# Folding the two half-masked key blocks of a windowed attention into one square

## The chip, the cores and the metric

The kernel runs on one core of a Trainium2 chip. The time is device time in microseconds; the kernel before took 1605.19 us (median of three runs, 1604.76 to 1605.27). One more execution was profiled; its trace is what is read below. Of the engines, TensorE (PE; its weight loads are PEld) multiplies matrices, VectorE (DVE), ScalarE (ACT) and GpSimd (POOL) do the rest, and SyncE (SP) issues the transfers.

## The reference

Two transformer blocks in sequence, over 512 tokens of width 2048, in float32. The change touches the first block's attention alone: 32 query heads of width 64 in 4 key groups (8 heads each), a window of 128 tokens, query blocks of 128 tokens, a bias by distance and a sink in the softmax:

```
kj = jnp.arange(2 * L)[None, :]           # L = 128: the key block before, and the own one
dist = qi + L - kj
in_band = (dist >= 0) & (dist < SWA_WINDOW)
s = jnp.einsum('bqhgd,bkhd->bhgqk', qj, kb) * scale + bias
s = jnp.where(in_band & (start - L + kj >= 0), s, -jnp.inf)
m = jnp.maximum(jnp.max(s, axis=-1, keepdims=True), sink)
p = jnp.exp(s - m)
p = p / (jnp.sum(p, axis=-1, keepdims=True) + jnp.exp(sink - m))
o = jnp.einsum('bhgqk,bkhd->bqhgd', p, vb)
```

For query i the window takes keys j <= i of the own block and keys j > i of the block before. So at each place (i, j) of a 128x128 square exactly one of the two blocks counts, and the other is masked.

## The kernel before

Every product is made of float32 numbers split in a high and a low half (`split`, lines 266 to 274: ACT writes the high half, VectorE the rest a moment later, as a "post"). Three matmuls (high x high, high x low, low x high) make one product.

Block 1 runs as one stream of projections on TensorE. `proj_n` goes over the 16 slices of 128 rows of a weight matrix; each step of three matmuls into one of four PSUM banks (`pj`) is a unit. The weights come in by DMA as `raw`, ACT converts them to `wh`, VectorE to `wl`, up to four slices ahead. First the projection of k and v (banks `kv_ps`), then four of q (`swa_q(g)`, from line 595, one for each key group), then the gate (`gate1(c)`).

The attention of group g is fed into the stream as pieces (`swa_pieces`, from line 638), so many for each unit (`F.rate`), while q of the next group is projected. An item is a group g, a query block t (0 to 3) and half of the heads (i): 32 items of 4 heads. Its pieces are: `s1` (twice: scores of two heads against 256 keys in a PSUM tile `sc`; VectorE adds the bias, takes the minimum `nm` and writes `p`; ACT takes exp and the row sum), `norm` (VectorE scales p by 1/sum), `s2` for each of the two key blocks (TensorE transposes four heads of p into a PSUM tile `tp`; the split makes `pth` and `ptl`), and `s3` (the products with v, bank `pv`, two matmuls a key block, the halves of v side by side; then the output goes to memory by DMA). `s3` of an item comes two pieces after its `s2`. At t = 0 there is only the own block.

The q of a group is normed after its bank is done (`evac`): ACT copies it (`qn`) and squares it, VectorE sums, GpSimd makes 1/sqrt (`rsqrt_mean`: `st`, a tensor_scalar and a pow) and multiplies (line 612). These are four norms for each group, one for each t; much later, ACT and VectorE split the result, TensorE transposes it, and `qt` is ready for `s1`.

ACT runs in the order of the program. For the other engines a scheduler lays the instructions in an order when the program is built; on the chip each engine then runs its own list in order and waits at whatever is not ready.

When the first bank of the gate is done (`gate1`, c = 0), all pieces that are left are issued, the attention's memory is closed, and the outputs are read back (`oin`) to be multiplied by the gate.

Of the kernel before, what the change touches and what calls it, by code (L numbers as in the profile page):

```python
# [9 lines left out]
F32 = mybir.dt.float32  # L10
# [10 lines left out]
NTB = 4  # L21
# [14 lines left out]
def mixer_kernel(ctx, tc, x, rel_bias, w_in1, q_gain, k_gain, sinks, w_out1,  # L36
# [483 lines left out]
    ktl = p1.tile([128, 4, S], F32R, name="ktl")  # L520
    vt = [p1.tile([128, 4, 2, 64], F32R, name=f"v{t}") for t in range(NTB)]

    def hstat():
# [7 lines left out]

    kn_all = p1.tile([128, 4, 256], F32, tag="p", name="kn_all", bufs=2)
    for t in range(NTB):
        ps = kv_ps[t]
        nc.scalar.activation(out=kn_all[:, t, :], in_=ps[:, 0:256], func=ACTF.Copy, scale=rstd1[:, t:t + 1])
        split(vt[t][:, :, 0, :], vt[t][:, :, 1, :], ps[:, 256:512].rearrange("p (g d) -> p g d", g=4),
              rstd1[:, t:t + 1])

    def k_norm(t):
        kn = kn_all[:, t, :]  # L540
        kn3 = kn.rearrange("p (g d) -> p g d", g=4)
        sq = qn_t()
        nc.scalar.activation(out=sq[:, :256], in_=kn, func=ACTF.Square)
# [94 lines left out]
    def swa_pieces():  # L638
# [3 lines left out]
        def s1(n, j):  # L642
# [20 lines left out]
            for a in range(2):  # L663
                b = 2 * j + a
                nc.vector.tensor_tensor_reduce(  # L665
                    out=p[:, b, :w], in0=sc[:, a, :w], in1=back(bias, b, w), scale=1.0,
                    scalar=nsink[:, h0 + b:h0 + b + 1], op0=ALU.add, op1=ALU.min,
                    accum_out=nm[:, b:b + 1])
                nc.scalar.activation(out=p[:, b, :w], in_=p[:, b, :w], func=ACTF.Exp, scale=-1.0,  # L669
                                     bias=nm[:, b:b + 1], accum_out=sm[:, b:b + 1])  # L670
# [6 lines left out]
        def norm(n):  # L677
            g, t, i = items[n]
            w = 128 if t == 0 else 256
            p, es, sm = st[n]["p"], st[n]["es"], st[n]["sm"]  # L680
            nc.vector.tensor_tensor(out=es, in0=es, in1=sm, op=ALU.add)
            nc.vector.reciprocal(out=es, in_=es)
            for b in range(4):
                nc.vector.tensor_scalar(out=p[:, b, :w], in0=p[:, b, :w], scalar1=es[:, b:b + 1],
                                        scalar2=None, op0=ALU.mult)

        def s2(n, kb):
            g, t, i = items[n]
            if kb == 0:
                st[n]["pth"] = p1.tile([128, 2, 512], F32R, tag="pth", name="pth", bufs=1)  # L690
                st[n]["ptl"] = p1.tile([128, 2, 512], F32R, tag="ptl", name="ptl", bufs=1)
            tp = tpt()
            for b in range(4):
                nc.tensor.transpose(tp[:, b, :], st[n]["p"][:, b, kb * 128:(kb + 1) * 128], ident)  # L694
            split(st[n]["pth"][:, kb, :], st[n]["ptl"][:, kb, :], tp.rearrange("p a b -> p (a b)"))

        def s3(n):
            g, t, i = items[n]
            h0 = 8 * g + 4 * i
            nk = 1 if t == 0 else 2  # L700
            k0 = max(t - 1, 0)
            pth, ptl = st[n]["pth"], st[n]["ptl"]
            o = ps_tp.tile([128, 512], F32, tag="tp", name="pv")
            for kb in range(nk):
                v = vt[k0 + kb][:, g].rearrange("p a b -> p (a b)")
                mm(o, v, pth[:, kb, :], kb == 0, False)
# [19 lines left out]
        for n in range(N + 2):  # L726
# [14 lines left out]
            if prev:  # L741
                out_p.append((None, lambda n=n: s2(n - 1, 0)))
            if prev and items[n - 1][1] > 0:
                out_p.append((None, lambda n=n: s2(n - 1, 1)))
        return out_p

    swa_bias(0)
    F.feed(swa_pieces())
    F.rate = 0.6
    for g in range(4):  # L750
# [43 lines left out]
    for t in range(NTB):  # L794
        F.defer(12 + t, lambda t=t: row_bcast(rb2[:, t * 128:(t + 1) * 128], rstd1[:, t:t + 1]))
    F.rate = 1.1
    phase({ACT})
# [789 lines left out]
```

## Time and profile before

| what | value |
|---|---|
| median of three runs | 1605.19 us (1604.76 to 1605.27) |
| the profiled execution | 1604.56 us, its span 1602.8 us |
| PE busy in the span | 1585.7 us, 99% |
| DVE, ACT, POOL busy | 917.8, 727.9, 110.1 us |
| chain that ended last | PE 91%, DVE 4%, ACT 2%, DMA 1%, issue 1% |
| granted TensorE clock | 0.999 of full speed |

The profile's page gives busy times of one execution. A matmul's own duration overlaps that of the next one; what a matmul adds to a full TensorE is the step from its start to the next start, which the chain of waits shows. A group of instructions is named by its line, engine, output and inputs. An "idle before" with a name says what the engine waited for.

### The profile page before, as it was taken

Reading aid. Unit: us, or ns where it says so; the run is one execution under the profiler, and the core shown is the slowest. Engines: PE = TensorE matmul, PEld = TensorE weight load, DVE = VectorE, ACT = ScalarE, POOL = GpSimd, SP = SyncE. Lnnn points to the kernel's source line nnn. Section 1 sums busy time; section 2 is a strip of 40 time slices with the busy share of each in tenths; the row PEclk is TensorE's granted clock in tenths of the full one; section 3 lists DMA queues with packets and bytes.
Section 4 is the critical chain, followed back from the end, with each engine's and each line's share of the span. In section 5 each row is a group of like instructions: output and inputs, shape, how many; then the busy total and the mean of one; then the engine's idle time right before and its main releaser. Section 6 shows DMA issues by size and latency. Waiting matters only on the chain.

```text
span 1602.8 us, 23242 instructions
## 1 busy us (share of the span) xinstructions
PE 1585.7 (99%) x8615; PEld 1358.8 (85%) x8615; DVE 917.8 (57%) x2218; ACT 727.9 (45%) x1608; POOL 110.1 (7%) x165
## 2 busy tenths in 40 slices
PE   9999999999999999999999999999999999999998
PEld 7788888887888788888899999999999888888887
DVE  6658888887454333333666766656657455455332
ACT  5556766775333323333455454545545333334322
POOL 3330320300000000000100000000000000000001
PEclk9999999999999999999999999999999999999999
DMA  6422323325333534342332322232232364365312
GB/s 231 146 79 83 104 81 96 84 69 171 120 104 104 161 123 142 110 134 67 80 96 67 92 71 79 74 86 76 57 106 66 109 203 127 95 221 173 105 40 106
DMA packets 144674, 173.78 MB, mean 108 GB/s; under 512 B 13088, under 2 KB 82080, under 8 KB 144032
## 3 DMA queue, kind: packets, MB, share of 16 engines
q1 hardware_dynamic: 144560, 172.29, 35.1%
q8 instruction: 68, 1.11, 0.3%
q14 instruction: 46, 0.38, 0.1%
HBM read 155.41 MB, written 16.84 MB: 107 GB/s over the span
## 4 chain that ended last, share of the span: by engine, by line
PE 91%; DVE 4%; ACT 2%; DMA 1%; issue 1%; POOL 0%; SPq 0%; ACTq 0%; POOLq 0%; DVEq 0%
PE pj L111 78%; PE sc L111 4%; PE pv L111 4%; PE tp L694 1%; PE tp L1290 1%; DMA xt<-in_x_t_dram 1%; DVE wl L168 1%; PE tp L622 1%; PE tp L425 0%; DVE xl L274 0%; PE sqs L1344 0%; PE ck_m L111 0%; ACT p L669 0%; DVE dql L272 0%; ACT wh L158 0%
## 5 line engine op out<-in xcount | busy, mean ns | idle before, releaser
L168 DVE TENSOR_TENSOR wl<-raw,wh 128x512 fp32r<-128x512 f32 (+1 forms) x488 | 336.0, 695 | 404.9 <-ACT wh L158 403.0
L158 ACT ACTIVATE wh<-raw 128x512 fp32r<-128x512 f32 (+1 forms) x488 | 298.6, 619 | 401.4 <-PE pj L111 351.4
L111 PE MATMUL pj<-xh,wh 128*128 128x512 f32 (+1 forms) x1152 | 363.6, 352 | 0.0
L111 PE MATMUL pj<-xh,wl 128*128 128x512 f32 (+1 forms) x1152 | 356.5, 345 | 0.6 <-DVE wl L168 0.6
L111 PE MATMUL pj<-xl,wh 128*128 128x512 f32 (+1 forms) x1152 | 356.3, 345 | 0.0
L111 PEld LDWEIGHTS pj<-xh,wh 128*128 128x128 f32 x1152 | 205.5, 188 | 27.8 <-ACT wh L158 0.4
L111 PEld LDWEIGHTS pj<-xh,wl 128*128 128x128 f32 x1152 | 199.7, 188 | 27.6 <-DVE wl L168 1.0
L111 PEld LDWEIGHTS pj<-xl,wh 128*128 128x128 f32 x1152 | 199.9, 188 | 19.5
L111 PE MATMUL pj<-wh,ogh 128*128 128x512 f32 (+1 forms) x528 | 204.6, 388 | 0.0
L111 PE MATMUL pj<-wl,ogh 128*128 128x512 f32 (+1 forms) x528 | 203.7, 386 | 0.0
L111 PE MATMUL pj<-wh,ogl 128*128 128x512 f32 (+1 forms) x528 | 203.6, 386 | 0.0
L111 PE MATMUL pj<-wh,xh 128*128 128x512 f32 (+1 forms) x448 | 175.3, 391 | 0.9 <-DVE v L274 0.7
L111 PE MATMUL pj<-wh,xl 128*128 128x512 f32 (+1 forms) x448 | 171.1, 382 | 1.2 <-DVE xl L274 1.1
L111 PE MATMUL pj<-wl,xh 128*128 128x512 f32 (+1 forms) x448 | 170.5, 380 | 0.1
L1253 ACT ACTIVATE p2t<-p2t,nm 128x144 f32<-128x144 f32 (+3 forms) x96 | 55.2, 575 | 140.0 <-DVE nm L1249 139.9
L111 PEld LDWEIGHTS pj<-wh,ogl 128*128 128x128 f32 x528 | 99.2, 188 | 21.3
L111 PEld LDWEIGHTS pj<-wh,ogh 128*128 128x128 f32 x528 | 99.2, 188 | 20.8
L111 PEld LDWEIGHTS pj<-wl,ogh 128*128 128x128 f32 x528 | 99.2, 188 | 20.7
L111 PEld LDWEIGHTS pj<-wh,xl 128*128 128x128 f32 x448 | 84.1, 188 | 18.8 <-DVE xl L274 2.9
L111 PEld LDWEIGHTS pj<-wh,xh 128*128 128x128 f32 x448 | 84.2, 188 | 13.9 <-DVE v L274 1.1
L111 PEld LDWEIGHTS pj<-wl,xh 128*128 128x128 f32 x448 | 84.3, 188 | 12.1 <-DVE wl L168 0.5
L669 ACT ACTIVATE p<-p,nm 128x256 f32<-128x256 f32 (+1 forms) x128 | 60.7, 475 | 60.6 <-DVE nm L665 60.5
(308 smaller groups left out, 2075.9 us busy)
## 6 DMA issues: line engine op xcount, KB each, us to landing
raw<-in_swa_w_in_dram SPq DMA_DIRECT2D x72, 512.0 KB, 3.7
raw<-in_w_in_dram SPq DMA_DIRECT2D x56, 512.0 KB, 3.8
raw<-in_swa_w_out_dram SPq DMA_DIRECT2D x32, 512.0 KB, 3.7
raw<-in_w_in_dram SPq DMA_DIRECT2D x128, 128.0 KB, 2.6
raw<-in_w_out_dram SPq DMA_DIRECT2D x32, 512.0 KB, 3.6
oin<-ot_d SPq DMA_DIRECT2D x8, 1024.0 KB, 7.1
bias<-bm_d SPq DMA_DIRECT2D x8, 512.0 KB, 4.9
ot_d<-ot SPq DMA_DIRECT2D x32, 128.0 KB, 1.8
```

Source lines behind the costliest of these rows:

```text
L111: nc.tensor.matmul(o, lhsT=l, rhs=r, start=start, stop=stop)
L158: nc.scalar.activation(out=h[:, :n], in_=self.raw_t[r][:, o:o + n], func=ACTF.Copy)
L168: nc.vector.tensor_tensor(out=l[:, :n], in0=self.raw_t[r][:, o:o + n], in1=f32(h[:, :n]), op=ALU.subtract)
L622: nc.tensor.transpose(tp[:, h, :].bitcast(F32R), qs[:, 4 * i + h].rearrange("p a b -> p (a b)"), identr)
L669: nc.scalar.activation(out=p[:, b, :w], in_=p[:, b, :w], func=ACTF.Exp, scale=-1.0, bias=nm[:, b:b + 1], accum_out=sm[:, b:b + 1])
L694: nc.tensor.transpose(tp[:, b, :], st[n]["p"][:, b, kb * 128:(kb + 1) * 128], ident)
L1253: nc.scalar.activation(out=p[:, :w], in_=p[:, :w], func=ACTF.Exp, scale=-1.0, bias=m, accum_out=sums[:, comp:comp + 1])
L1290: nc.tensor.transpose(tp[:, kb, :], p[:, kb * 128:(kb + 1) * 128], ident)
```

## The change

For t > 0 the scores of both key blocks are still made, biased and written to `p` (256 wide). Then VectorE takes the elementwise minimum of the two 128-wide halves (the scores are negated and masked ones are huge, so the minimum is the one that counts), and exp, row sum and scaling work on 128 columns. One transposed block remains for the item, with one split. The product with v becomes: all of the square times the own block's v, plus the strictly lower-left part (key above query in the transposed square) times the difference of the v of the block before and the own one. That second operand is made by GpSimd: an `affine_select` copies `pth` (and, as a post, `ptl`) with zeros where the own block counts. The differences `vd` are made and split once for each t > 0. For that, k and v leave PSUM together in one 512-column copy for each t, and v is split later from the copy. The numbers of pieces for each unit go from 0.6 to 0.52 and from 1.1 to 0.95.

```diff
--- before.py
+++ after.py
@@ -519,6 +519,7 @@
     kth = p1.tile([128, 4, S], F32R, name="kth")
     ktl = p1.tile([128, 4, S], F32R, name="ktl")
     vt = [p1.tile([128, 4, 2, 64], F32R, name=f"v{t}") for t in range(NTB)]
+    vd = [None] + [p1.tile([128, 4, 2, 64], F32R, name=f"vd{t}") for t in range(1, NTB)]
 
     def hstat():
         return p1.tile([128, 8], F32, tag="st", name="st", bufs=4)
@@ -529,17 +530,33 @@
     def qs_t():
         return p1.tile([128, 8, 2, 64], F32R, tag="qs", name="qs", bufs=4)
 
-    kn_all = p1.tile([128, 4, 256], F32, tag="p", name="kn_all", bufs=2)
+    kvn = []
     for t in range(NTB):
-        ps = kv_ps[t]
-        nc.scalar.activation(out=kn_all[:, t, :], in_=ps[:, 0:256], func=ACTF.Copy, scale=rstd1[:, t:t + 1])
-        split(vt[t][:, :, 0, :], vt[t][:, :, 1, :], ps[:, 256:512].rearrange("p (g d) -> p g d", g=4),
-              rstd1[:, t:t + 1])
+        kvn.append(qn_t())
+        nc.scalar.activation(out=kvn[t], in_=kv_ps[t], func=ACTF.Copy, scale=rstd1[:, t:t + 1])
+
+    def v3(t):
+        return kvn[t][:, 256:512].rearrange("p (g d) -> p g d", g=4)
+
+    def v_split(t):
+        split(vt[t][:, :, 0, :], vt[t][:, :, 1, :], v3(t))
+
+    def v_diff(t):
+
+        d = p1.tile([128, 512], F32, tag="sq", name="vdf", bufs=1)
+        d3 = d[:, :256].rearrange("p (g d) -> p g d", g=4)
+        nc.vector.tensor_tensor(out=d3, in0=v3(t - 1), in1=v3(t), op=ALU.subtract)
+        split(vd[t][:, :, 0, :], vd[t][:, :, 1, :], d3)
+
+    for t in range(NTB):
+        F.defer(1 + 8 * t, lambda t=t: v_split(t))
+        if t:
+            F.defer(2 + 8 * t, lambda t=t: v_diff(t))
 
     def k_norm(t):
-        kn = kn_all[:, t, :]
+        kn = kvn[t][:, 0:256]
         kn3 = kn.rearrange("p (g d) -> p g d", g=4)
-        sq = qn_t()
+        sq = p1.tile([128, 512], F32, tag="sq", name="ksq", bufs=1)
         nc.scalar.activation(out=sq[:, :256], in_=kn, func=ACTF.Square)
         st = hstat()
         nc.vector.tensor_reduce(out=st[:, :4], in_=sq[:, :256].rearrange("p (g d) -> p g d", g=4),
@@ -666,7 +683,13 @@
                     out=p[:, b, :w], in0=sc[:, a, :w], in1=back(bias, b, w), scale=1.0,
                     scalar=nsink[:, h0 + b:h0 + b + 1], op0=ALU.add, op1=ALU.min,
                     accum_out=nm[:, b:b + 1])
-                nc.scalar.activation(out=p[:, b, :w], in_=p[:, b, :w], func=ACTF.Exp, scale=-1.0,
+            if t:
+                wr = p[:, 2 * j:2 * j + 2]
+                nc.vector.tensor_tensor(out=wr[:, :, 0:128], in0=wr[:, :, 0:128],
+                                        in1=wr[:, :, 128:256], op=ALU.min)
+            for a in range(2):
+                b = 2 * j + a
+                nc.scalar.activation(out=p[:, b, :128], in_=p[:, b, :128], func=ACTF.Exp, scale=-1.0,
                                      bias=nm[:, b:b + 1], accum_out=sm[:, b:b + 1])
             if j == 1:
                 es = p1.tile([128, 4], F32, tag="es", name="es", bufs=3)
@@ -675,34 +698,40 @@
                 nc.scalar.activation(out=es, in_=es, func=ACTF.Exp)
 
         def norm(n):
-            g, t, i = items[n]
-            w = 128 if t == 0 else 256
             p, es, sm = st[n]["p"], st[n]["es"], st[n]["sm"]
             nc.vector.tensor_tensor(out=es, in0=es, in1=sm, op=ALU.add)
             nc.vector.reciprocal(out=es, in_=es)
             for b in range(4):
-                nc.vector.tensor_scalar(out=p[:, b, :w], in0=p[:, b, :w], scalar1=es[:, b:b + 1],
+                nc.vector.tensor_scalar(out=p[:, b, :128], in0=p[:, b, :128], scalar1=es[:, b:b + 1],
                                         scalar2=None, op0=ALU.mult)
 
-        def s2(n, kb):
+        def s2(n):
+
             g, t, i = items[n]
-            if kb == 0:
-                st[n]["pth"] = p1.tile([128, 2, 512], F32R, tag="pth", name="pth", bufs=1)
-                st[n]["ptl"] = p1.tile([128, 2, 512], F32R, tag="ptl", name="ptl", bufs=1)
+            pth = p1.tile([128, 2, 512], F32R, tag="pth", name="pth", bufs=1)
+            ptl = p1.tile([128, 2, 512], F32R, tag="ptl", name="ptl", bufs=1)
+            st[n]["pth"], st[n]["ptl"] = pth, ptl
             tp = tpt()
             for b in range(4):
-                nc.tensor.transpose(tp[:, b, :], st[n]["p"][:, b, kb * 128:(kb + 1) * 128], ident)
-            split(st[n]["pth"][:, kb, :], st[n]["ptl"][:, kb, :], tp.rearrange("p a b -> p (a b)"))
+                nc.tensor.transpose(tp[:, b, :], st[n]["p"][:, b, 0:128], ident)
+            split(pth[:, 0, :], ptl[:, 0, :], tp.rearrange("p a b -> p (a b)"))
+
+            def before(a):
+                nc.gpsimd.affine_select(out=a[:, 1, :], in_=a[:, 0, :],
+                                        compare_op=ALU.is_gt, fill=0.0, base=0,
+                                        pattern=[[0, 4], [-1, 128]], channel_multiplier=1)
+            if t:
+                before(pth)
+                F.post(lambda: before(ptl))
 
         def s3(n):
             g, t, i = items[n]
             h0 = 8 * g + 4 * i
             nk = 1 if t == 0 else 2
-            k0 = max(t - 1, 0)
             pth, ptl = st[n]["pth"], st[n]["ptl"]
             o = ps_tp.tile([128, 512], F32, tag="tp", name="pv")
             for kb in range(nk):
-                v = vt[k0 + kb][:, g].rearrange("p a b -> p (a b)")
+                v = (vd if kb else vt)[t][:, g].rearrange("p a b -> p (a b)")
                 mm(o, v, pth[:, kb, :], kb == 0, False)
                 mm(o, v, ptl[:, kb, :], False, kb == nk - 1)
             tmp = p1.tile([64, 4, 128], F32, tag="otmp", name="otmp", bufs=1)
@@ -739,14 +768,12 @@
             if cur:
                 out_p.append((None, lambda n=n: s1(n, 1)))
             if prev:
-                out_p.append((None, lambda n=n: s2(n - 1, 0)))
-            if prev and items[n - 1][1] > 0:
-                out_p.append((None, lambda n=n: s2(n - 1, 1)))
+                out_p.append((None, lambda n=n: s2(n - 1)))
         return out_p
 
     swa_bias(0)
     F.feed(swa_pieces())
-    F.rate = 0.6
+    F.rate = 0.52
     for g in range(4):
         swa_q(g)
 
@@ -793,7 +820,7 @@
 
     for t in range(NTB):
         F.defer(12 + t, lambda t=t: row_bcast(rb2[:, t * 128:(t + 1) * 128], rstd1[:, t:t + 1]))
-    F.rate = 1.1
+    F.rate = 0.95
     phase({ACT})
     for c in range(4):
         gate1(c)
```

Where instructions move: GpSimd's list at the q norms of the third group, before. The names are `st` (statistics of one t) and `qn` (the copied q); the list goes on with the fourth norm.

```order
L106 TENSOR_SCALAR st_2421<-st_2421 128x8
L108 TENSOR_TENSOR st_2421<-st_2421,mhalf_80 128x8
L612 TENSOR_TENSOR qn_2417<-qn_2417,st_2421 128x512
L106 TENSOR_SCALAR st_2454<-st_2454 128x8
L108 TENSOR_TENSOR st_2454<-st_2454,mhalf_80 128x8
L612 TENSOR_TENSOR qn_2450<-qn_2450,st_2454 128x512
L106 TENSOR_SCALAR st_2478<-st_2478 128x8
L108 TENSOR_TENSOR st_2478<-st_2478,mhalf_80 128x8
L612 TENSOR_TENSOR qn_2474<-qn_2474,st_2478 128x512
```

The same place after. `pth` and `ptl` belong to the item that is multiplied next.

```order
L106 TENSOR_SCALAR st_2415<-st_2415 128x8
L108 TENSOR_TENSOR st_2415<-st_2415,mhalf_80 128x8
L629 TENSOR_TENSOR qn_2411<-qn_2411,st_2415 128x512
L106 TENSOR_SCALAR st_2448<-st_2448 128x8
L108 TENSOR_TENSOR st_2448<-st_2448,mhalf_80 128x8
L629 TENSOR_TENSOR qn_2444<-qn_2444,st_2448 128x512
L106 TENSOR_SCALAR st_2472<-st_2472 128x8
L108 TENSOR_TENSOR st_2472<-st_2472,mhalf_80 128x8
L629 TENSOR_TENSOR qn_2468<-qn_2468,st_2472 128x512
L720 AFFINE_SELECT pth_2493<-pth_2493 128x512
L720 AFFINE_SELECT ptl_2494<-ptl_2494 128x512
```

Two selects now stand behind the three norms, and the fourth norm (`st_2513`) stands behind them.

TensorE's list at the product with v of the item in that place, before (second group, t = 2, second half of the heads).

```order
L111 MATMUL sc_2590<-kth_565,qt_1982 128x256
L111 MATMUL pv_2572<-pth_2510,v1_568 128x512
L111 MATMUL pv_2572<-ptl_2511,v1_568 128x512
L111 MATMUL pv_2572<-pth_2510,v2_569 128x512
L111 MATMUL pv_2572<-ptl_2511,v2_569 128x512
L111 MATMUL sc_2590<-ktl_566,qt_1982 128x256
L111 MATMUL sc_2590<-kth_565,qt_1982 128x256
L111 MATMUL sc_2590<-ktl_566,qt_1982 128x256
```

The same product for that item after; `vd2` is the difference for t = 2, `pj_2517` a bank of the next q projection.

```order
L111 MATMUL pj_2517<-wh_2358,xl1_94 128x512
L111 MATMUL pv_2557<-pth_2493,v2_569 128x512
L111 MATMUL pj_2517<-wh_2399,xh1_93 128x512
L111 MATMUL pj_2517<-wl_2406,xh1_93 128x512
L111 MATMUL pj_2517<-wh_2399,xl1_94 128x512
L111 MATMUL pv_2557<-ptl_2494,v2_569 128x512
L111 MATMUL pv_2557<-pth_2493,vd2_572 128x512
L111 MATMUL pv_2557<-ptl_2494,vd2_572 128x512
L111 MATMUL pj_2518<-wh_2358,xh1_93 128x512
```

The four pv stood together; now three pj matmuls stand between the first and the other three. Between the last matmul of the q bank whose norm is the first one shown (`pj_1759`) and the pv that reads `vd2` with `pth` stand 31 pj, 12 sc, 6 pv and one group of four transposes.

TensorE's list where the attention ends, before: the last pv and the first gate column (`pj_3340` to `pj_3342`). Seven more matmuls of this column lie between the last row shown and the next column (`pj_4272`).

```order
L111 MATMUL pj_3340<-xh1_93,wh_4104 128x512
L111 MATMUL pv_4207<-pth_4179,v3_570 128x512
L111 MATMUL pj_3340<-xl1_94,wh_4104 128x512
L111 MATMUL pj_3340<-xh1_93,wl_4123 128x512
L111 MATMUL pv_4207<-ptl_4180,v3_570 128x512
L111 MATMUL pj_3341<-xh1_93,wh_4031 128x512
L111 MATMUL pj_3341<-xl1_94,wh_4031 128x512
L111 MATMUL pj_3341<-xh1_93,wl_4050 128x512
L111 MATMUL pj_3341<-xh1_93,wh_4104 128x512
L111 MATMUL pj_3341<-xl1_94,wh_4104 128x512
```

The same place after; `pj_4218` is the next column.

```order
L111 MATMUL pv_4145<-ptl_4126,v3_570 128x512
L111 MATMUL pv_4145<-pth_4125,vd3_573 128x512
L111 MATMUL pv_4145<-ptl_4126,vd3_573 128x512
L111 MATMUL pj_3322<-xh1_93,wl_4009 128x512
L111 MATMUL pj_3322<-xh1_93,wh_4059 128x512
L111 MATMUL pj_3322<-xl1_94,wh_4059 128x512
L111 MATMUL pj_3322<-xh1_93,wl_4079 128x512
L111 MATMUL pj_4218<-xh1_93,wh_4118 128x512
L111 MATMUL pj_4218<-xl1_94,wh_4118 128x512
```

The last pv stood twelve pj matmuls ahead of the next column and now stands four ahead.

## Rows read from the trace of the kernel before

**Rows 1.** The page: busy us (share) and instructions of each engine.
```profile
PE 1585.7 (99%) x8615; PEld 1358.8 (85%) x8615; DVE 917.8 (57%) x2218; ACT 727.9 (45%) x1608; POOL 110.1 (7%) x165
```

**Rows 2.** Busy by stretch: length, PE, PEld, DVE, ACT, POOL, clock, DMA share, GB/s.
```profile
60.00:112.00 52.00, 52.00 (x251) 42.97 (x251) 25.80 (x46) 23.17 (x44) 14.27 (x18) 1.00 0.36 104
112.00:360.00 248.00, 247.06 (x1370) 206.40 (x1368) 208.94 (x661) 172.51 (x468) 39.23 (x38) 1.00 0.29 85
```

**Rows 3.** Operations, 80 to 375 us: busy, mean ns, idle before.
```profile
L272 DVE TENSOR_TENSOR ptl<-tp,pth 128x512 fp32r<-128x512 f32 x56 | 37.8, 684 | 2.5 <-ACT pth L268 2.3
L694 PE MATMUL tp<-identr,p 128*128 128x128 f32 x224 | 35.7, 273 | 0.0
L684 DVE TENSOR_SCALAR p<-p,es 128x256 f32<-128x256 f32 x96 | 30.5, 357 | 0.6
L612 POOL TENSOR_TENSOR qn<-qn,st 128x512 f32<-128x512 f32 x16 | 17.8, 1112 | 1.3
L600 ACT ACTIVATE qn<-pj,rstd 128x512 f32<-128x512 f32 x16 | 10.9, 680 | 0.8 <-PE pj L111 0.7
L684 DVE TENSOR_SCALAR p<-p,es 128x128 f32<-128x128 f32 x32 | 7.8, 281 | 0.3
L557 DVE TENSOR_TENSOR qs<-kn_all,qs 128x256 fp32r<-128x256 f32 x2 | 0.8, 421 | 0.5 <-ACT qs L555 0.5
```

**Rows 4.** Chain that ended last, one item: start, us added, what.
```profile
200.04 0.44 PE tp L694 x4
200.47 1.39 PE pj L111 x6
201.87 0.47 PE sc L111 x4
```

**Rows 5.** Timeline of PE at the first q projection: start, us.
```profile
55.20 0.39 PE L111 MATMUL pj<-wh,xl 128*128 128x512 f32 x1
56.28 0.50 PE L111 MATMUL pj<-wh,xh 128*128 128x512 f32 x1 [0.69 <-DVE v L274]
```

**Rows 6.** Timeline of ACT there.
```profile
54.81 0.47 ACT L535 ACTIVATE kn_all<-pj,rstd 128x256 f32<-128x256 f32 x1 [2.23 <-POOL rstd L108]
```

**Rows 7.** Operations of POOL, whole span.
```profile
L1071 POOL MEMSET dql<- 128x512 f32 x2 | 1.0, 517 | 0.0
masks.py:199 POOL TENSOR_SCALAR_AFFINE_SELECT eye<-eye 128x128 f32<-128x128 f32 x1 | 0.3, 293 | 0.1
```

**Rows 8.** Timeline of POOL, fourth multiply of a burst.
```profile
175.82 1.38 POOL L612 TENSOR_TENSOR qn<-qn,st 128x512 f32<-128x512 f32 x1
```

**Rows 9.** Timeline of POOL, last burst, first and fourth norm.
```profile
297.63 0.20 POOL L106 TENSOR_SCALAR st<-st 128x8 f32<-128x8 f32 x1 [56.09 <-DVE st L606]
...
307.60 0.20 POOL L106 TENSOR_SCALAR st<-st 128x8 f32<-128x8 f32 x1
```

**Rows 10.** Timeline of ACT, first q copy of that burst.
```profile
295.06 0.69 ACT L600 ACTIVATE qn<-pj,rstd 128x512 f32<-128x512 f32 x1
```

**Rows 11.** Timeline of PE, one group of transposes.
```profile
216.65 0.60 PE L694 MATMUL tp<-identr,p 128*128 128x128 f32 x4
```

**Rows 12.** Timeline of DVE, the low half from that group.
```profile
218.32 0.69 DVE L272 TENSOR_TENSOR ptl<-tp,pth 128x512 fp32r<-128x512 f32 x1
```

**Rows 13.** Timeline of DVE beside the multiply of rows 8.
```profile
176.22 1.39 DVE L684 TENSOR_SCALAR p<-p,es 128x256 f32<-128x256 f32 x2
```

**Rows 14.** Chain that ended last, at the handover to the gate.
```profile
374.17 0.26 PE pv L111
...
388.74 0.61 DVE wl L168
...
389.40 5.74 PE pj L111 x24
```

**Rows 15.** Timeline of DVE there.
```profile
383.11 1.29 DVE L762 SCALAR_TENSOR_TENSOR gs<-oin,gs 128x512 f32<-128x512 f32 x2 [2.08 <-DMA oin<-ot_d]
```

## The prediction

> **What bounds the kernel now.** I read the page's busy times first: TensorE is busy for 1585.7 of 1602.8 us [rows 1], so time is won only by taking work off TensorE, and lost by anything that makes it wait. Then the busy times by stretch: the change lies in block 1, and between 112 and 360 us, where the windowed attention runs inside the q projections, TensorE is busy for 247.1 of 248 us, VectorE for 208.9 and GpSimd for 39 [rows 2]. The reader should see two things: TensorE has no slack there, and VectorE (84%) has not much. Last come the rows of single operations, for prices, and the timelines of three places: GpSimd's burst of q norms, the start of the q projections and the handover to the gate.
>
> The profiled execution took 1604.56 us (span 1602.8 and 1.76 around it), the median of the three timed runs is 1605.19. I sum against the first and add the result to the second.
>
> **Off TensorE.** One transposed block of probabilities replaces two in the 24 items with t > 0: 96 of 224 transposes go [rows 3], and every other matmul keeps its count and shape (the difference pass is a pv matmul like the one that it replaces). Their mean of 273 ns overlaps; the chain shows what a group of four adds to a packed TensorE, 0.44 us, where six pj matmuls take 1.39 (0.232 each) and four sc 0.47 [rows 4]. 24 x 0.44 = **-10.5 us**.
>
> **The start of the q projections.** TensorE stands 0.69 us for the low half of v, which was the last reader of the first kv bank [rows 5]. Now one 512-column copy frees it; the first copy began at 54.81 [rows 6] and such a copy takes 0.68 (L600) [rows 3], so TensorE resumes near 55.6 and not at 56.28: **-0.7**. The new splits and the three differences of v come later, each some 0.42 (L557, same size) [rows 3]; between 60 and 112 us ACT and VectorE are busy for 23 and 26 of 52 us [rows 2] and the weights are converted ahead, so I count them at nothing (2 us if a conversion were late each time).
>
> **VectorE and ACT in an item.** VectorE loses 24 ptl (16 us) and 96 x (357 - 281) ns = 7 us of scaling, and gains 48 folds of 2x128, 0.42 at most: 20 us. Net -3 us [rows 3]. So VectorE stays as busy while the stretch shrinks. ACT gets lighter. The value 0 for both is hidden under TensorE; the fold stands in the chain of an item, ahead of exp, where the exp is waited for by no matmul for some microseconds.
>
> **GpSimd, the price that no row shows.** 48 affine selects of 128x512 enter a queue that had none. Nearest rows: a 128x128 select took 0.293, a 512-column memset 0.517 [rows 7], the 512-column tensor multiply L612 1.11 on average [rows 3]. Bounds: 0.52 below, 4 x 0.293 = 1.17 by size, 1.38 when VectorE is in the way [rows 8]. I take 1.05, near the multiply.
>
> What counts is where they stand in the queue. In the order of after, three q norms (st, pow, multiply) of the next group stand ahead of both selects of the item whose differences are multiplied next; this is so in two groups (the selects of pth_2493 and of pth_3293), and in the first group one and then two norms stand between. GpSimd runs in order. In the burst at 297 us the fourth norm starts 9.97 us after the first [rows 9], so three norms take that long. The first can start 2.57 us after ACT begins to copy the projected q (295.06) [rows 9, 10], and the copy some 0.4 us (one matmul's duration [rows 5]) after the bank's last matmul has issued. So the high half is ready at 0.4 + 2.6 + 10.0 + 1.05 = 14.0 us after that matmul. TensorE's order puts 31 pj, 12 sc, 6 pv and one group of transposes between that matmul and the first pv that reads the half: 31 x 0.232 + 12 x 0.118 + 6 x 0.235 + 0.44 = 10.4 us [rows 4]. Wait 3.5 us; the low half comes 1.1 later and its pv 0.23 later: 0.9 more. About 4.3 us, twice. Everything queued behind the pv on TensorE (the pj and sc of other items) waits too, and nobody gives it back, since TensorE is the bound. In the first group the same working (ACT's pth after the q copy and square, one norm of 3.1, one select) gives 7.7 against a place at 6.7, then 0.4 at the next item: 1.4. **Bursts: +10.0** (8 at 0.8 us a select, 12.5 at 1.4).
>
> **The other selects.** In before, the low half was ready 2.4 us after its transposes began (216.65 to 219.01) [rows 11, 12]; another 1.15 to 1.6 for the select and its queueing makes 3.5 to 4.1. By the order, TensorE reaches the last pv 3.9 to 5.1 us after the group's start in the other items, 3.5 in the last one. Few and small waits: **+1.5** (0 to 9 with selects of 1.4 that wait for VectorE each time).
>
> **Contention.** Beside the multiply of 175.82 us two scalings on VectorE took 1.39 us [rows 8, 13], where two take 0.71 (357 each) [rows 3]: one was held by 0.7 us. Forty-eight more GpSimd reads, most beside an operation of that kind, hold VectorE by 0.2 to 0.7 us each, 10 to 34 us, of which I let **+1.5** reach TensorE (0 to 10). The Trainium skill says the same ("SBUF — State Buffer", section "Who interferes with whom"): a VectorE instruction with two SBUF inputs, and a scaling in its two-port mode, shares an exclusive lock with a GpSimd instruction that reads SBUF, and the loser waits for the whole instruction. By that rule each select can cost a full 1.05 us, 50 us in all, and VectorE would be the bound; the row's 0.7 is nearer to it than to nothing. That is the slower rival below.
>
> **The handover to the gate.** After the last pv (374.17) its output is stored, read back as oin and multiplied; ACT runs in order and holds the next weights behind that, and TensorE stands until 389.40 [rows 14]. VectorE had waited 2.08 us for oin [rows 15]. Twelve pj of the first gate column follow the last pv in before, four in after. TensorE arrives 8 x 0.232 = 1.9 us earlier at the same wait: **+1.8** (0 to 3). The two new rates set this spacing and issue nothing.
>
> Waits that TensorE has in this stretch already (0.9 of 248 us) [rows 2] partly fall into the new ones: **-0.5**.
>
> **Sum.** -10.5 - 0.7 + 10.0 + 1.5 + 1.5 + 1.8 - 0.5 = +3.1; 1604.56 + 3.1 = 1607.7 by the profiled execution, 1605.19 + 3.1 = 1608 by the median. The transposes are really saved and are paid back as waits for GpSimd.
>
> **Rivals.**
> - Slower: VectorE becomes the bound. Place: each item's fold, scaling and weight conversion, held by the selects. It decides from a hold of 0.7 us on: 34 us more on 206 leaves VectorE as busy as TensorE's 237, and each late half makes pv wait; selects of 1.4 go with it. +2.5 in the bursts, +7 at the other items: some 1618. For it: the 1.39 us row; the lock of the Trainium skill ("SBUF — State Buffer", above) would bring it. Against: the multiply's neighbours are mostly not that much longer (a mean of 357 for the scalings).
> - Faster: the waits in the bursts do not come, because GpSimd is ahead there (selects near 0.5 us and norms that start as soon as the copy is made). Then -10.5 - 0.7 + 1.8 = -9.4: 1596. For it: TensorE's order was laid so that pv comes late. Against: three norms of 3.1 us are measured, and they stand ahead in the queue.
>
> **Chances.** The forecast with its own range, 1602 to 1612: 0.61. The slower rival: 0.24. The faster: 0.15. A measurement of this kernel tells 0.2% (3.2 us) from no change, so bounds at 1602 and 1608.4: the forecast's case gives 0.07 faster, 0.36 within, 0.18 slower. Together 0.22, 0.36, 0.42. The range 1598 to 1617 leaves out most of the faster case (0.1) and half of the slower (0.1).
>
> **What the profile of after would show.** 128 transposes of p, no wait at 55.4; selects of about 1 us; in two bursts a pv that waits some 3.5 us for the select and then 0.9; TensorE idle in 112 to 360 near 13 us, against 0.9; a wait of near 3 us at the handover. Wrong if pv hardly waits in the bursts (then near 1596), or if selects last 1.5 us and more, or VectorE's idle time is gone (then 1615 and over).

## The result and the profile after

The changed kernel takes 1619.55 us (median of 4 runs, 1618.89 to 1619.81), the kernel before 1604.97 beside it (4 runs): 14.6 us slower, ratio 1.009 with a 95% interval of 1.0077 to 1.0102. The forecast was 1608, its range 1598 to 1617.

The same instruction in both traces shows how much of it is block 1. First the matmul that waited for a low half of x, ahead of everything that changed, then the one that waits for mrstd, behind the gate; before first (columns: start us, us, instruction, idle before):

```profile
49.36 0.50 PE L111 MATMUL pj<-wh,xl 128*128 128x512 f32 x1 [0.34 <-DVE xl L274]
...
535.11 0.39 PE L432 MATMUL rbps<-identr,mrstd 16*128 16x16 f32 x2 [0.75 <-POOL mrstd L108]
```

and after:

```profile
48.89 0.50 PE L111 MATMUL pj<-wh,xl 128*128 128x512 f32 x1 [0.31 <-DVE xl L274]
...
549.55 0.39 PE L432 MATMUL rbps<-identr,mrstd 16*128 16x16 f32 x2 [0.75 <-POOL mrstd L108]
```

From -0.47 to +14.44: 14.9 us come in between, and the rest of the kernel runs as it did. The page and the stretches that answer to [rows 1, 2], in their columns:

```profile
PE 1586.2 (98%) x8519; PEld 1351.8 (84%) x8519; DVE 922.0 (57%) x2248; ACT 707.3 (44%) x1587; POOL 147.3 (9%) x213
```

```profile
60.00:112.00 52.00, 52.00 (x256) 43.07 (x255) 28.72 (x55) 25.76 (x51) 16.07 (x18) 1.00 0.36 110
112.00:360.00 248.00, 235.05 (x1221) 190.18 (x1220) 199.96 (x645) 143.51 (x420) 66.92 (x76) 0.98 0.27 79
...
243.00:246.00 3.00, 3.00 (x9) 2.31 (x10) 0.83 (x2) 0.60 (x1) 2.75 (x4) 0.50 0.41 148
246.00:249.00 3.00, 3.00 (x10) 2.31 (x10) 1.60 (x8) 1.24 (x6) 0.47 (x1) 0.50 0.35 76
...
318.00:321.00 3.00, 3.00 (x9) 2.28 (x8) 2.18 (x4) 1.58 (x6) 2.65 (x2) 0.54 0.63 178
```

TensorE is idle for 12.95 of 248 us, as forecast (13). But look at the column of the clock (the third from the end): at two places it falls to about 0.50, which is 1.2 GHz, and a stretch at that clock counts as busy in full with half the matmuls in it (10 in 3 us, where 16 to 22 are usual). That is one part of why the page's TensorE time stands at 1586.2 although 96 transposes are gone; the other is gaps too short to be shown as idle, counted below. Busy is not work.

The operations that answer to [rows 3], 80 to 390 us (busy, mean ns, idle before):

```profile
L705 DVE TENSOR_SCALAR p<-p,es 128x128 f32<-128x128 f32 x128 | 32.5, 302 | 0.8
...
L688 DVE TENSOR_TENSOR p<-p 128x256 f32<-128x256 f32 x48 | 23.1, 480 | 0.8
...
L716 PE MATMUL tp<-identr,p 128*128 128x128 f32 x128 | 20.7, 276 | 0.0
...
L720 POOL TENSOR_SCALAR_AFFINE_SELECT ptl<-ptl 128x512 fp32r<-128x512 f32 x24 | 18.2, 759 | 3.8 <-DVE ptl L272 3.4 <-PE pj L111 0.2
...
L720 POOL TENSOR_SCALAR_AFFINE_SELECT pth<-pth 128x512 fp32r<-128x512 f32 x24 | 15.8, 660 | 192.4 <-ACT pth L268 175.0 <-DVE wl L168 17.4
```

A select takes 0.66 to 0.76 us, less than the 1.05 taken. Then the second burst, on GpSimd (idle times over 0.2 stand in brackets):

```profile
231.81 0.20 POOL L106 TENSOR_SCALAR st<-st 128x8 f32<-128x8 f32 x1 [1.03 <-DVE es L703]
232.09 1.73 POOL L108 TENSOR_TENSOR st<-st,mhalf 128x8 f32<-128x8 f32 x1
233.90 1.05 POOL L629 TENSOR_TENSOR qn<-qn,st 128x512 f32<-128x512 f32 x1
...
240.59 1.58 POOL L629 TENSOR_TENSOR qn<-qn,st 128x512 f32<-128x512 f32 x1
242.12 0.63 POOL L720 TENSOR_SCALAR_AFFINE_SELECT pth<-pth 128x512 fp32r<-128x512 f32 x1
242.71 0.63 POOL L720 TENSOR_SCALAR_AFFINE_SELECT ptl<-ptl 128x512 fp32r<-128x512 f32 x1
```

and on TensorE at the same time:

```profile
238.08 0.39 PE L111 MATMUL pv<-ptl,v 128*128 128x512 f32 x1
242.81 0.79 PE L111 MATMUL pv<-pth,vd 128*128 128x512 f32 x1 [4.34 <-POOL pth L720]
243.40 0.79 PE L111 MATMUL pv<-ptl,vd 128*128 128x512 f32 x1
243.99 0.63 PE L111 MATMUL pj<-wh,xh 128*128 128x512 f32 x1
```

Three norms hold GpSimd for 10.3 us, the select stands behind them, pv behind the select: the place and nearly the price that the prediction gave. What it did not have is the last three rows: behind the wait the matmuls take 0.63 to 0.79 us, not 0.39. All waits of TensorE in 80 to 400 us (total, times, longest):

```profile
PE pv L111 <- POOL pth L720: 8.2, 2, 4.3
PE pv L111 <- POOL ptl L720: 3.6, 4, 2.4
PE pj L111 <- DVE gs L784: 2.0, 1, 2.0
PE tp L639 <- DVE qs L272: 0.3, 1, 0.3
```

### The profile page after: what moved, and what is told of

Same layout as the page of the kernel before. It is cut to its first block, busy times and chain, and to the rows that moved or that the text cites. A ratio compares the mean times of both kernels' runs of the same rounds, so it can differ in the third digit from the quotient of the medians.

```text
span 1617.5 us, 23151 instructions
## 1 busy us (share of the span) xinstructions
PE 1586.2 (98%) x8519; PEld 1351.8 (84%) x8519; DVE 922.0 (57%) x2248; ACT 707.3 (44%) x1587; POOL 147.3 (9%) x213
## 4 chain that ended last, share of the span: by engine, by line
PE 86%; DVE 6%; ACT 3%; DMA 2%; issue 1%; POOL 1%; SPq 0%; ACTq 0%; POOLq 0%; DVEq 0%
PE pj L111 74%; PE sc L111 4%; PE pv L111 3%; DVE wl L168 1%; DMA xt<-in_x_t_dram 1%; PE tp L1317 1%; DVE p L682 1%; ACT p L692 1%; PE tp L639 1%; DVE ot L745 1%; DVE p L688 1%; PE tp L716 1%; DVE ptl L272 0%; DMA oin<-ot_d 0%; PE tp L425 0%
## 5 line engine op out<-in xcount | busy, mean ns | idle before, releaser
L111 PEld LDWEIGHTS pj<-wl,xh 128*128 128x128 f32 x448 | 84.7, 189 | 12.1
L692 ACT ACTIVATE p<-p,nm 128x128 f32<-128x128 f32 x128 | 50.5, 395 | 89.2 <-DVE p L688 71.6
```

What stands on the lines that cost most here:

```text
L111: nc.tensor.matmul(o, lhsT=l, rhs=r, start=start, stop=stop)
L692: nc.scalar.activation(out=p[:, b, :128], in_=p[:, b, :128], func=ACTF.Exp, scale=-1.0, bias=nm[:, b:b + 1], accum_out=sm[:, b:b + 1])
```

## Where the time went

The waits in brackets miss what a matmul loses in smaller pieces. So I took the start of each matmul in TensorE's timeline from the start of the next. Packed, one of 512 columns takes a place of 0.229 us, one of 256 columns 0.117, a transposed block of p 0.089. What is over is a gap, put down to the instruction behind it; in a stretch at half clock one place more goes to the clock. Between the same two pj matmuls (61.85 and 432.60 us in the kernel before) that gives, in us:

| kernel | stretch | transposes of p | gaps before pv | before the gate's pj | half clock | other gaps |
|---|---|---|---|---|---|---|
| before | 370.8 | 19.9 | 2.3 | 1.3 | 0 | 9.4 |
| after | 386.4 | 11.4 | 17.9 | 3.9 | 3.9 | 11.5 |
| after, old rates | 370.5 | 11.4 | 7.2 | 2.0 | 0 | 12.1 |
| before, new rates | 377.2 | 19.9 | 3.5 | 3.2 | 1.4 | 11.4 |
| after, no selects | 368.0 | 11.4 | 2.0 | 1.9 | 1.4 | 13.4 |
| after, q multiply on VectorE | 376.6 | 11.4 | 9.5 | 2.6 | 1.6 | 13.6 |
| after, old rates, pv later | 363.5 | 11.4 | 3.0 | 3.5 | 0 | 7.8 |

The rest of each stretch, 337.8 us, is the same work in all. From before to after: -8.5 by the places of the transposes, +15.6 before pv (11.1 of them in the three bursts: 2.6, 4.5 and 4.0), +3.9 by the clock, +2.5 at the handover, +2.1 in small gaps elsewhere, and -0.7 ahead of the stretch: 14.9. How the last three columns share what is left depends on which matmuls are counted to the handover; counted another way, up to 1.5 us move from one to another, and their sum stays.

The places hide one thing. The matmul behind a run of transposes is followed by the next one 0.31 us later and not 0.23, in both kernels. In the kernel before:

```profile
216.65 0.60 PE L694 MATMUL tp<-identr,p 128*128 128x128 f32 x4
217.01 0.48 PE L111 MATMUL pj<-wh,xh 128*128 128x512 f32 x1
217.32 0.40 PE L111 MATMUL pj<-wl,xh 128*128 128x512 f32 x1
```

The four blocks take 0.36 us from start to start and the step behind them 0.08 more, 0.44 in all. The kernel before has 70 such runs in the stretch (some of fewer blocks), the changed one 39. Counted with that step the transposes take 24.9 and 14.6 us: 10.3 less, and not 8.5. The small gaps elsewhere have then grown by 3.9 us, and not 2.1. Some 2.0 of these 3.9 are the same kind of step behind a wait, here in the changed kernel:

```profile
402.49 0.50 PE L111 MATMUL pj<-xh,wh 128*128 128x512 f32 x1 [0.88 <-ACT wh L158]
402.82 0.40 PE L111 MATMUL pj<-xl,wh 128*128 128x512 f32 x1
```

The step is 0.33 us again, 0.1 too long. It stands behind each of 23 gaps of 0.12 us and more that the changed kernel has at full clock, and the kernel before has 5 of them. What the other 1.9 us depend on is open.

## Experiments

Each is an edit of the changed kernel, unless it says otherwise; the ratio is to the kernel before, timed beside it, with its 95% interval.

**1. The selects left out.** What does everything that hangs on them cost?

```diff
-            if t:
-                before(pth)
-                F.post(lambda: before(ptl))
...
-                mm(o, v, pth[:, kb, :], kb == 0, False)
-                mm(o, v, ptl[:, kb, :], False, kb == nk - 1)
+                mm(o, v, pth[:, 0, :], kb == 0, False)
+                mm(o, v, ptl[:, 0, :], False, kb == nk - 1)
```

> Leaves out the selects: the difference pass reads the unselected halves, so the mask between the two key blocks is missing from the result. All else is as in the changed kernel. Queue theory (pv waits for selects that stand behind q norms in GpSimd's queue, and the granted clock falls after the long waits): the gaps ahead of pv go back to the 2 us that they had before, no stretch at clock 0.5 between 112 and 400 us, and what stays is the shorter transposes, the start and the handover: 1605 - 9 + 3 = 1599. Rival, lock theory (the selects hold VectorE by the port they share): 1599 too, but with VectorE's own operations measurably shorter than with selects. Rival, spacing theory (the two new rates and the fold in the item's chain are what costs): most of the loss stays, 1612 to 1616.

Measured 1600.45, ratio 0.9976 (0.9967 to 0.9986). The spacing theory, as I had put it, falls: with the same rates the whole loss goes when the selects go, and 4 us more. The hold on VectorE is small. Without selects VectorE's fold and scaling take, in 110 to 375 us,

```profile
L705 DVE TENSOR_SCALAR p<-p,es 128x128 f32<-128x128 f32 x128 | 31.3, 293 | 0.8
...
L688 DVE TENSOR_TENSOR p<-p 128x256 f32<-128x256 f32 x48 | 20.2, 421 | 0.8
```

against 302 and 480 with them: 128 x 9 + 48 x 59 ns = 4 us on an engine with slack. Even that is not fixed by the number of selects: with the same 48 of them the fold takes 435 and 424 ns in experiments 7 and 11.

**2. GpSimd in program order.** The norm's multiplies come behind the selects of the first long wait.

```diff
-    phase({ACT})
+    phase({ACT, mybir.EngineType.Pool})
```

> GpSimd's instructions keep program order in block 1, nothing else is edited. In the group whose burst stood at 237 us, only the three scalings and powers (1.9 us each) now stand ahead of the selects, the three 1.2 us multiplies come after; in the last group the multiplies still stand ahead. Queue theory: the wait of 4.3 us goes with its clock fall (3.4 us), the one of 3.8 us in the last group stays: 1611 to 1613. Lock theory: the number of selects and multiplies is the same, so nothing changes: 1618 to 1620.

Measured 1617.28, ratio 1.0076 (1.0059 to 1.0093): in neither range, and nearer to that of the lock theory. The wait of 4.34 went as the queue theory had it, 0.48 and 0.28 are left in its place, and the one of 3.82 stayed; but the multiplies, now late, made others. Two rows of TensorE:

```profile
180.29 0.34 PE L639 MATMUL tp<-identr,qs 128*128 128x128 f32 x1 [2.65 <-DVE qs L272]
...
241.53 0.49 PE L111 MATMUL pv<-pth,vd 128*128 128x512 f32 x1 [0.48 <-POOL pth L720]
```

The first is a transpose of q, which waits for a late norm; behind it, too, the clock fell (0.60 in 181 to 184 us). The queue theory holds for the place, not for the time. It missed that whoever is put back in the queue has a reader as well.

**3. The q norm's multiply on VectorE.**

```diff
-                nc.gpsimd.tensor_tensor(out=qn3, in0=qn3, ...
+                nc.vector.tensor_tensor(out=qn3, in0=qn3, ...
```

> The q norm's 128x512 multiply goes from GpSimd to VectorE (16 of them); the scaling and the power stay. Queue theory: three norms then hold GpSimd for 5.6 us and not 10, the high half is ready some 9.3 us after the last matmul of the bank against a place at 10.4, so both long waits go and both clock falls with them: 1619.6 - 11 - 5 = 1603 to 1605. Lock theory: VectorE is the tight engine, and gets 16 x 0.7 = 11 us more: 1620 or above.

Measured 1609.42, ratio 1.0029 (1.0018 to 1.004). Both long waits are down to 0.48 and the clock stays at 1.00 through the q projections; with 11 us more work on VectorE the kernel is 10 us faster than the changed one, which the lock theory, as put, excludes. The gain is less than expected by 5: two waits for VectorE came at the first norms (1.55 and 1.19), the small waits before pv stayed, and the clock fell once at the handover (1.6 us in the table).

**4. The selects as VectorE multiplies** by a square of zeros and ones (`msk`, made once ahead of the block).

```diff
-                nc.gpsimd.affine_select(out=a[:, 1, :], in_=a[:, 0, :], ...
+                nc.vector.tensor_tensor(out=a[:, 1, :] ..., in0=f32(a[:, 0, :]) ...,
+                    in1=msk.unsqueeze(1).to_broadcast([128, 4, 128]), op=ALU.mult)
```

> The two selects of an item become two VectorE multiplies by a 0/1 square; GpSimd has the q norms alone, as before. Adds 48 x 0.7 = 33 us to VectorE. Queue theory: no long wait for GpSimd and no clock fall, but VectorE goes from 39 to near 46 of 50 us, so low halves come late more often: 1603 to 1610. Lock theory: VectorE, already the bound, gets more: 1620 and above. Spacing theory: no change, 1617 to 1620.

Measured 1612.02, ratio 1.0046 (1.0031 to 1.0061), 2 us above the range of the queue theory. VectorE is busy for 227.7 of 248 us in the stretch, 28 more than in the changed kernel, and still the time falls. So VectorE is not the bound of the changed kernel. It became tight here: TensorE waits for six kinds of its results and three of ACT's, the longest time 2.9 at the handover. And the clock, which that theory had staying up, fell at two places near it, the first time behind waits of only 0.20, 0.73 and 0.23 us:

```profile
366.00:369.50 3.50, 2.34 (x9) 0.97 (x7) 3.50 (x15) 2.00 (x6) 0.00 (x0) 1.00 0.00 0
369.50:373.00 3.50, 3.50 (x10) 2.86 (x11) 3.02 (x10) 1.57 (x6) 0.00 (x0) 0.51 0.31 64
```

**5. Matmuls in place of the two long waits.**

```diff
+            if n in (13, 21):
+                for _ in range(18):
+                    mm(o, identr, pth[:, 0, :], True, True)
```

> Ahead of the pv of the two items that waited 4.34 and 3.82 us, 18 matmuls of an identity into the same bank are added (4.2 us each time, overwritten by the real pass): TensorE works in place of waiting, nothing else changes. Clock theory (the granted clock of 0.5 behind these two waits was brought by them and cost 3.9 us on its own): no stretch at 0.5 between 112 and 400 us, the waits are filled, and the time is 1619.6 - 3.9 + 0.3 = 1616. Rival (the clock falls for another reason, or the selects are late because TensorE is): the fall stays or the wait comes behind the added matmuls, 1619 to 1624.

Measured 1618.11, ratio 1.0088 (1.0073 to 1.0103), between the two expectations. TensorE by stretch (the clock is the third from the end):

```profile
168.00:172.00 4.00, 3.54 (x11) 2.80 (x12) 1.95 (x4) 0.75 (x2) 3.59 (x6) 0.57 0.47 157
243.00:252.00 9.00, 8.36 (x42) 6.79 (x43) 5.22 (x15) 4.25 (x11) 5.62 (x7) 1.00 0.47 131
316.00:325.00 9.00, 8.15 (x40) 6.64 (x41) 5.53 (x15) 4.25 (x11) 5.83 (x8) 1.00 0.25 73
389.00:394.00 5.00, 4.27 (x12) 3.40 (x13) 4.96 (x9) 3.39 (x6) 0.00 (x0) 0.66 0.85 229
```

Where the waits were filled, the clock stays at 1.00, so those two falls hung on the waits. But it fell at two other places, behind waits of 2.42 (first burst) and 2.01 us (handover), where the changed kernel has waits of 2.44 and 2.02 and no fall. The clock still cost some 3 us in this run by the same working, so the time says little: that the falls follow waits is shown, their full price by itself is not.

**6. The pv piece one piece later.**

```diff
-            if n >= 2:
-                out_p.append((None, lambda n=n: s3(n - 2)))
             if cur:
                 out_p.append((None, lambda n=n: s1(n, 1)))
+            if n >= 2:
+                out_p.append((None, lambda n=n: s3(n - 2)))
```

> The pv piece of an item comes one piece later, behind the next item's second pair of scores; some 1.8 us later. Queue theory: the 19 small waits for the low half (4.5 us over those of the bursts) go, the three burst waits of 2.4, 4.3 and 3.8 us shrink by 1.8 each, the clock falls become shorter: 1619.6 - 4.5 - 5.4 - 2 = 1608. Rival, VectorE theory (the late halves come from a late chain on VectorE, so that whatever is moved later only meets the next wait): no gain, 1617 to 1620.

Measured 1611.23, ratio 1.0043 (1.0027 to 1.006), 3 us above the queue theory. The small waits went; the long ones shrank less than expected (2.06 and 3.45 are left), and each still brought the clock down, as did a wait of 2.93 at the handover, where the changed kernel has 2.02 and no fall.

**7. The old rates.**

```diff
-    F.rate = 0.52
+    F.rate = 0.6
...
-    F.rate = 0.95
+    F.rate = 1.1
```

> Only the two rates go back to 0.6 and 1.1; with four pieces an item in place of five, the items then come faster than in the kernel before. Spacing theory (the lower rates cost the handover and the rest): 1612 to 1615. Queue theory: items come 13% faster, each pv has less time to its select, so the waits grow, and the handover comes earlier in the gate's first column, where more matmuls are left to cover it: gains and losses of 2 to 4 us, 1617 to 1623.

Measured 1604.71, ratio 1.0003 (0.9994 to 1.0013). Both expectations are wrong: two numbers that issue no instruction carry the whole loss. GpSimd and TensorE at the same place as above:

```profile
230.58 0.88 POOL L720 TENSOR_SCALAR_AFFINE_SELECT pth<-pth 128x512 fp32r<-128x512 f32 x1 [6.10 <-ACT pth L268]
231.69 0.70 POOL L720 TENSOR_SCALAR_AFFINE_SELECT ptl<-ptl 128x512 fp32r<-128x512 f32 x1 [0.23 <-DVE ptl L272]
232.58 0.20 POOL L106 TENSOR_SCALAR st<-st 128x8 f32<-128x8 f32 x1 [0.19 <-DVE es L702]
...
241.90 1.09 POOL L720 TENSOR_SCALAR_AFFINE_SELECT pth<-pth 128x512 fp32r<-128x512 f32 x1
```

```profile
231.95 0.39 PE L111 MATMUL pv<-pth,vd 128*128 128x512 f32 x1
232.44 0.50 PE L111 MATMUL pv<-ptl,vd 128*128 128x512 f32 x1
...
246.09 0.40 PE L111 MATMUL pv<-pth,vd 128*128 128x512 f32 x1
```

The norms run at the same time as in the changed kernel (from 232.6, there 231.8). But the item whose selects stood behind three of them there (index 13) has its selects done at 232.4, just ahead. The next item's select is now the one behind three norms (241.90); its pv comes only at 246.09, since its piece is queued behind one that needs the next group's q, the product of these very norms. The burst falls into a pause that the items make anyway. An item takes 4 / 0.52 = 7.7 units of three matmuls in the changed kernel and 6.7 with the old rate, and a group of q 64 units: eight items of 7.7 fill 62 of them and leave next to no pause, eight of 6.7 leave nearly eleven units.

**8. Both pieces, pv later and the q norm's multiply on VectorE.**

> The later pv piece together with the q norm's multiply on VectorE. Queue theory: no wait for a select is left in the bursts or beside them, pv gaps near 2 us as in the kernel before; left are the waits at the first q norms (2.7 us) and at the handover: 1609.4 - 7 = 1602 to 1604, just under the kernel before. VectorE theory: no better than the multiply's move alone, 1609 to 1612.

Measured 1613.29, ratio 1.0055 (1.004 to 1.007): worse than either alone, and above both ranges. The waits for selects are down to 1.2 us, and in their place TensorE waits for VectorE (the outputs ot 3.8, qs 2.1, gs 2.9), with two falls of the clock. At the low rate another operand was late next, which is what the VectorE theory had said.

**9. Only the first rate back** (0.6, the gate's stays at 0.95).

> Only the rate of the q projections goes back to 0.6; the gate's stays at 0.95. Phase theory (the first rate decides which item's selects come behind the norms of the next bank: at 0.6 the item with index 13 has its selects ahead of them, at 0.52 behind three of them): the long waits and the clock falls stay away as with both rates back, and only the handover is as in the changed kernel: 1605 to 1608. Rival (the second rate, by the handover and the last items): 1615 or above.

Measured 1606.1, ratio 1.0011 (1.0002 to 1.002), in the range of the phase theory. The long waits for selects stay away; the clock fell once, at the handover (0.57 in 377 to 381 us), where that theory had no fall. By the medians the first rate is worth 13.5 us, the second 1.4.

**10. The kernel before with the new rates.**

```diff
-    F.rate = 0.6
+    F.rate = 0.52
...
-    F.rate = 1.1
+    F.rate = 0.95
```

> The kernel before with the two new rates alone. With five pieces an item it then falls behind, so more items are left for the gate's first column. Phase theory (the rates cost by way of the selects alone, and the kernel before has none): no long wait for GpSimd in the q projections, only the handover moves: 1604 to 1609. Rival (the rates cost whatever the items wait for): 1612 to 1618.

Measured 1610.81, ratio 1.0034 (1.0021 to 1.0047): between the two expectations. No wait for GpSimd, but the items, with five pieces, lag, and the handover is met with less to cover it:

```profile
383.30 0.80 PE L111 MATMUL pj<-xh,wh 128*128 128x512 f32 x1 [2.35 <-DVE gs L757]
```

The 0.80 shows the clock down behind that wait as well. So the rates cost 6 us without the fold, the fold nothing measurable without the rates, both together 14.6: by subtraction some 8 us are of the two meeting, the selects at that rhythm.

**11. The old rates and the later pv.**

> Both rates back and the pv piece one piece later. Queue theory: the pv gaps left with the rates back, 7.2 us against 2.3 before, are small waits for the low half, and go: 1604.7 - 4.5 = 1600 to 1601, which would beat both kernels. Rival (another operand is late next, as with the later piece at the low rate): 1604 to 1606.

Measured 1595.47, ratio 0.9939 (0.9927 to 0.9952): it beats both kernels, by more than expected. TensorE's waits in 80 to 400 us are all in three rows:

```profile
PE pj L111 <- DVE gs L784: 1.6, 1, 1.6
PE pj L111 <- DVE wl L168: 1.1, 1, 1.1
PE pv L111 <- POOL ptl L720: 0.9, 1, 0.9
```

The gaps before pv are back at 3.0, and the saved transposes are kept. Here the small gaps elsewhere fell too, by 4; what they hung on I did not test.

**12. Rates of 0.68 and 1.25.**

> Rates of 0.68 and 1.25, over those of the kernel before by as much as its items have fewer pieces. GpSimd's order then has the selects of the items 13 and 21 two places ahead of the norms, and those of 14 and 22 around the first norm. Phase theory: no long wait, but each pv comes sooner after its selects (small waits up by 2 to 3 us), the handover covered better (down 1 to 2): 1604 to 1607. Rival (shorter spacing only is better): 1600 to 1602. Third (the small waits add up): 1610.

Measured 1602.91, ratio 0.9988 (0.998 to 0.9997): between the range of the phase theory and that of its rival. No long wait for a select (the longest 0.3), but 3.3 us for weights around the handover. The three points are 1619.6, 1604.7 and 1602.9 at 0.52, 0.6 and 0.68. By these times alone a shorter spacing could simply be better; that it is the order of selects and norms rests on the rows of experiment 7.

## Why the prediction was wrong

By its own steps, in us:

| step | predicted | measured |
|---|---|---|
| transposes, with the step behind them | -10.5 | -10.3 |
| start of the q projections | -0.7 | -0.7 |
| bursts | +10.0 | +11.1 |
| other selects and contention, before pv | +3.0 | +4.5 |
| handover | +1.8 | +2.5 |
| granted clock | not in the sum | +3.9 |
| other small gaps, old waits | -0.5 | +3.9 |
| sum | +3.1 | +14.9 |

The step that failed is the price of a wait: the sum took it at its length alone, with nothing for what TensorE does behind it. In its place the runs show a fall of the clock behind the long waits (3.9 us) and a longer step behind each wait (2.0). The rest of the 11.8 us missed are terms a little too small, all in one direction.

- *Start.* Right: TensorE's matmul at the old wait of [rows 5] starts 0.35 after its neighbour, and its lead grows by 0.7.

```profile
54.74 0.39 PE L111 MATMUL pj<-wh,xl 128*128 128x512 f32 x1
55.09 0.50 PE L111 MATMUL pj<-wh,xh 128*128 128x512 f32 x1
```

- *Bursts.* Right in mechanism, place and nearly in size: waits of 4.34 and 3.82 for the high half against 3.5, and 2.44 (for a low half) in the first group, where 1.4 was forecast. The selects were cheaper than taken, the norms a little longer (10.3 us for three). The 0.9 for the low half behind each long wait did not come, so that the total was nearly met partly by luck.
- *Transposes.* Right: -10.3 against -10.5. The 0.44 a group of the chain [rows 4] holds the 0.36 of the four blocks and the 0.08 of the step behind them.
- *Handover.* Somewhat mis-sized: waits of 2.02, 0.88 and 0.62 there (390.43, 402.49, 403.84) against "near 3 us" in all. The longest was not the wait that was named: at 390.43 TensorE waits for VectorE's `gs` (L784), which reads the bank that the next matmul writes, and not for the weights behind ACT. And "TensorE stands until 389.40" misreads the chain of before: 60 pj ran from 374.43 on, and TensorE stood for 0.61.
- *The clock* is the largest term that was missing. I priced a wait at its length. The trace of before showed the clock at 1.00 through the stretch [rows 2], and I took that as given, though the sum itself put waits of several us into an engine that had had none. Behind both long waits the rows show 1.2 GHz. The Trainium skill says so ("TensorE: Matmul & The Clock Gate", section "HAM oscillation — how this bites in real kernels"): a wait for data can throttle the array, and the work behind it then starts cold; this trace agrees, with 0.50 at 243 to 249 us behind a wait of 4.34. By that sentence, at this run's price, the forecast would have been 4 us higher: 1612, still 7.5 short of the measured time.
- *Small gaps* were put at -0.5 and came out at +3.9, the largest miss of a term. Some 2.0 of them are the step of 0.33 us behind a wait; waits came at some twenty places, where the sum had a few. The other 1.9 are open.
- *The rates.* "The two new rates set this spacing and issue nothing", and I used them for the handover alone. The runs show that they decide which selects stand behind the norms: with them put back, 1604.71. The bursts that I took for the price of the fold are the price of its rhythm (experiments 7 and 9); the order after showed the queue, and I did not ask what had set it.
- *Rivals.* The slower one came near in time (1618) for a reason that the runs refute: VectorE was busy for 200 of 248 us, and work given to it made the kernel faster (experiments 3 and 4). By the lock rule of the Trainium skill ("SBUF — State Buffer", section "Who interferes with whom"), taken at its full price, 50 us were possible by the prediction's estimate; the fold's 480 against 421 ns and the scaling's 302 against 293 say that 4 came. The faster one was right in what it would take: without burst waits the fold is no loss, and with the small ones gone as well it is the gain of 9 us of experiment 11, where the rival had put 9.4. There the transposes with their step are down by 10.5 and the handover is up by 2.2, where it had 10.5 and 1.8.
- *Its own signs.* TensorE's idle time came out at 12.95 us against 13, while the time was 11.5 us off. A busy sum shows neither a slow clock nor gaps shorter than an instruction's tail.

## What to carry to other kernels

Work that runs in rhythm beside another loop is placed by its rate: when pieces are removed, go through the phases at two or three rates before judging the edit, and look for the rate that puts a burst on a shared queue into a pause. A wait on a TensorE that had none costs its length, a longer step behind it and, behind the long ones here, a stretch at half clock. When a saving disappears in a queue, making its reader later (here by one piece) can bring it back: 8 us at the low rate, 9 at the old ones. Making the queue shorter brought 10 at the low rate (experiment 3); at the old ones it was not run.

## What the runs showed of the hardware

- The affine select on GpSimd took 0.63 to 0.64 us for 128x512 at its shortest, and up to 1.09 beside VectorE's split of q (241.90, experiment 7); a 128x8 power there took 1.64 to 1.96 in the second burst of the changed kernel and of experiment 7, where the 128x512 multiply took 1.04 to 1.58: it is the largest part of a q norm.
- Behind waits of like length (2.44 and 2.42, 2.02 and 2.01 us) TensorE's clock fell in one run and not in the other. The falls behind the longer ones (4.34, 3.82, 3.45, 2.9) came each time, and in experiment 4 one came behind 0.20, 0.73 and 0.23.
- A matmul of 512 columns takes a place of 0.43 us at 1.2 GHz and 0.229 at 2.4. The step behind a wait is 0.33 at 2.4 GHz, the one behind a run of transposes 0.31.
